# The two softmaxes of an attention unit: maximum, negation and exponential one softmax at a time

## The chip, the cores and the metric

The kernel runs on one core of a Trainium2 chip. The metric is the device time of one execution in microseconds (us); lower is better. The core has five engines that run side by side, each working through its own list of instructions in order: TensorE (PE: matmuls, with its weight loads PEld), VectorE (DVE), ScalarE (ACT), GpSimd (POOL) and SyncE (SP, which issues most loads). An instruction that needs another engine's result waits at the head of its engine's list, and all behind it wait too.

## The reference, cut to what matters

Two layers are applied to 640 tokens (512 latent ones and 128 context ones, 1024 wide). Each layer normalizes, projects to nine groups of 256 columns, runs four mixers side by side (differential attention, a gated short convolution, a gated recurrence, pooling), concatenates them, projects back, and then runs a squared-ReLU MLP. The change is in the differential attention of the latent tokens:

```python
def block(qi):
    s1 = jnp.einsum('bhqd,bhkd->bhqk', qi[..., :DK], k1).astype(jnp.float32) * scale
    s2 = jnp.einsum('bhqd,bhkd->bhqk', qi[..., DK:], k2).astype(jnp.float32) * scale
    p = jax.nn.softmax(s1, axis=-1) - lam * jax.nn.softmax(s2, axis=-1)
    return jnp.einsum('bhqk,bhkd->bhqd', p.astype(v.dtype), v)
```

There are 4 heads and 4 blocks of 128 queries, each against 640 keys (128 cached, 512 new): 16 units per layer, 32 in all, and each has two softmaxes over 640 keys.

## The kernel before

One function, `attn_unit`, records a unit. Four matmuls (L793) write both score blocks into one PSUM tile `S` of 128 x 1536, of which columns 128 to 768 are the first softmax and 768 to 1408 the second; there is one such tile. VectorE takes both row maxima in one instruction (L802) and multiplies the two by minus the scale in one more (L803), into columns of a small tile `mx`. ScalarE computes the two exponentials with that as bias (L806), each with its row sum, into two buffers of the pool `e`, which has three. VectorE then combines them (L810, L811, and L813 over 640 columns), which frees one `e`. TensorE transposes the result (L820, L825), ScalarE copies that out of PSUM (L827, L828), and after every second unit TensorE multiplies with the values (L840) and VectorE copies the output to `osb` (L845). After all units `attn_gen` squares the outputs (L882), sums them on TensorE (L885), takes the norm (L887 to L892), spreads it (L903), transposes it (L907), multiplies (L910) and splits the two halves of the attention output, `y[0]` and `y[1]`, into a high and a low part (L911, L912).

The other mixers and the large matmuls (L583, groups of 24 matmuls per result tile) run beside this. The projections of a layer come as `xr`, `gc`, `xb`, `xp`, `gr`, `gb`, each in four groups (0A, 1A, 0B, 1B), and after them the output projection `o`, whose groups go through `y[0]` to `y[7]` in order: `y[0]` and `y[1]` are the attention, `y[5]` ends with L639, `y[7]` with L1063. Weights are split into a high part on ScalarE (L260) and a low part on VectorE (L243).

All these pieces are Python generators that one loop advances in turn, and which buffer each takes is settled there, in the same way before and after the change. The order of instructions on each engine is then settled by a scheduler, which also puts in the waits between engines.

Of the kernel before, what the change touches and what calls it, by code (L numbers as in the profile page):

```python
# [12 lines left out]
OP = mybir.AluOpType  # L13
AX = mybir.AxisListType
# [100 lines left out]
class Net:  # L115
# [666 lines left out]
    def attn_unit(self, l, h, qt):  # L782
        nc = self.nc
        sc = 32.0 ** -0.5
        i = 4 * qt + h
        while not self.psS.ok():
            yield
        ps = self.psS.get()
        st = self.stacks[h]
        for s, parts in ((0, ((128, 0, 384), (512, 384, 640))), (1, ((768, 0, 256), (1024, 256, 640)))):  # L790
            Q, K = st[s]
            for o, a, b in parts:
                nc.tensor.matmul(ps[:, o:o + b - a], Q[:, qt * P:(qt + 1) * P], K[:, a:b], start=True, stop=True)  # L793
        if qt == 3:
            for s in range(2):
                self.z.put(*st[s])
        yield
        while not self.e.ok(2):
            yield
        mx = self.mx[self.mxi % 4]  # L800
        self.mxi += 1
        nc.vector.tensor_reduce(mx[:, 0:2], ps[:, 128:1408].rearrange("p (s k) -> p s k", s=2), AX.X, OP.max)  # L802
        nc.vector.tensor_scalar(mx[:, 2:4], mx[:, 0:2], -sc, None, OP.mult)  # L803
        es = [self.e.get(), self.e.get()]
        for s in range(2):
            nc.scalar.activation(es[s], ps[:, 128 + 640 * s:768 + 640 * s], AF.Exp, bias=mx[:, 2 + s:3 + s],  # L806
                                 scale=sc, accum_out=self.sm[:, i, s:s + 1])
        self.psS.put(ps)
        yield
        nc.vector.reciprocal(mx[:, 4:5], self.sm[:, i, 1:2])  # L810
        nc.vector.scalar_tensor_tensor(mx[:, 5:6], self.sm[:, i, 0:1], mx[:, 4:5], self.small[l][:, 4:5],  # L811
                                       OP.mult, OP.mult)
        nc.vector.scalar_tensor_tensor(es[0], es[1], mx[:, 5:6], es[0], OP.mult, OP.add)  # L813
        self.e.put(es[1])
        yield
        while not self.psA.ok():
            yield
        ta = self.psA.get()
        for kt in range(4):
            nc.tensor.transpose(ta[:, kt * P:(kt + 1) * P], es[0][:, kt * P:(kt + 1) * P], self.ident)  # L820
        yield
        while not (self.psB.ok() and self.pt.ok(2 - h % 2)):
            yield
        tb, pT = self.psB.get(), self.pt.get()
        nc.tensor.transpose(tb[:, 0:P], es[0][:, 512:640], self.ident)  # L825
        self.e.put(es[0])
        nc.scalar.copy(pT[:, 0:512], ta)  # L827
        nc.scalar.copy(pT[:, 512:640], tb[:, 0:P])  # L828
        self.psA.put(ta)
        self.psB.put(tb)  # L830
        self.pTs[h % 2] = pT
        if h % 2 == 0:
            return
        yield
        while not (self.v_done and self.psB.ok()):
            yield
        tb = self.psB.get()
        for kt in range(5):
            for j in range(2):
                nc.tensor.matmul(tb[64 * j:64 * j + 64, 0:P], self.vsb[:, kt, (h - 1 + j) * 64:(h + j) * 64],  # L840
                                 self.pTs[j][:, kt * P:(kt + 1) * P], start=(kt == 0), stop=(kt == 4),
                                 tile_position=(0, 64 * j))
        self.pt.put(*self.pTs)
        yield
        nc.vector.tensor_copy(self.osb[:, h // 2, qt * P:(qt + 1) * P], tb[:, 0:P])  # L845
        self.psB.put(tb)
# [764 lines left out]
```

## Time and profile before

| | us |
|---|---|
| median of 3 runs | 1493.53 (1489.97 to 1493.6) |
| the profiled execution | 1486.77 |
| its span in the trace | 1484.9 |
| PE busy | 1451.9 (98%) |
| DVE busy | 941.2 (63%) |
| ACT busy | 596.9 (40%) |
| POOL busy | 61.1 (4%) |

The span is what the trace covers; 1.87 us lie around it. The shares are means over stages that differ: the mixers of the first layer lie at about 62 to 250 us, those of the second at about 780 to 967 us, and the rest is mostly MLP. PE's busy time is modelled for pipelined matmuls, so that its idle time and the granted clock (PEclk, 1.00 is full speed) of a stretch say more than its share.

### The profile page before, as it was taken

What the parts mean: (1) busy time and instruction counts of PE and PEld (TensorE: products, weight loads), DVE (VectorE), ACT (ScalarE), POOL (GpSimd) and SP (SyncE); (2) the same over time, 40 slices, a digit from 0 to 9 for tenths busy, and PEclk for the clock granted to TensorE, in tenths of its full rate; (3) what the DMA queues carried; (4) which work ended last, traced back from release to release, by engine and by line L of the source; (5) the groups of instructions that cost most, each with busy time, mean ns of one, the idle gap of its engine ahead of it and who ended that gap; (6) DMA issues with size and microseconds to landing.
All of it is one profiled execution on the core that took longest, in us unless ns stands there. A gap on an engine that the chain in (4) does not pass through costs nothing.

```text
span 1484.9 us, 24604 instructions
## 1 busy us (share of the span) xinstructions
PE 1451.9 (98%) x9991; PEld 1388.0 (93%) x9991; DVE 941.2 (63%) x1846; ACT 596.9 (40%) x1083; POOL 61.1 (4%) x104
## 2 busy tenths in 40 slices
PE   8989999999999999999999999899999999999998
PEld 6867988999999999999999888799999999999997
DVE  5645888898886677776467678948533433433453
ACT  5435884453224133123344588625412312312331
POOL 1230010010000000000002200000000000000000
PEclk9999999999999999999999999999999999999999
DMA  9596013435554444544235501121222222221211
GB/s 336 173 245 184 22 46 89 142 109 165 186 170 130 153 145 140 170 128 128 71 90 129 132 17 58 59 71 57 86 86 72 71 86 67 76 86 59 84 44 72
DMA packets 135961, 164.59 MB, mean 111 GB/s; under 512 B 10212, under 2 KB 111032, under 8 KB 135848
## 3 DMA queue, kind: packets, MB, share of 16 engines
q1 hardware_dynamic: 128184, 151.69, 33.2%
q0 software_dynamic: 4224, 6.45, 1.9%
q10 hardware_dynamic: 3440, 4.88, 1.3%
q8 instruction: 79, 1.29, 0.4%
q14 instruction: 34, 0.28, 0.1%
HBM read 150.40 MB, written 3.15 MB: 103 GB/s over the span
## 4 chain that ended last, share of the span: by engine, by line
PE 83%; DVE 5%; DMA 5%; issue 4%; ACT 2%; ACTq 0%; DVEq 0%; POOLq 0%
PE g_L_0A L583 14%; PE g_L_1A L583 14%; PE g_L_0B L583 14%; PE g_L_1B L583 14%; PE g_L_o_0A L583 2%; DMA st<-in_w_in 2%; PE g_L_o_0B L583 2%; PE g_L_o_1B L583 2%; PE g_L_o_1A L583 2%; PE U L949 1%; PE S L793 1%; PE TB L840 1%; PE TA L820 1%; DMA st<-in_w_ada 1%; PE S L1501 1%
## 5 line engine op out<-in xcount | busy, mean ns | idle before, releaser
L260 ACT CAST wh<-st 128x1024 fp32r<-128x1024 f32 x180 | 188.8, 1049 | 336.1 <-PE g_L_1B L583 273.7
L243 DVE TENSOR_TENSOR wl<-st,wh 128x1024 fp32r<-128x1024 f32 x176 | 215.0, 1222 | 118.0 <-ACT wh L260 117.3
L1280 DVE TENSOR_TENSOR e<-e 128x320 f32<-128x320 f32 x128 | 62.5, 489 | 111.3 <-ACT z L1277 111.0
L583 PE MATMUL g_L_0A<-z,wh 128*128 128x320 f32 (+1 forms) x512 | 120.5, 313 | 0.6 <-DVE x L1220 0.4
L583 PE MATMUL g_L_1A<-z,wh 128*128 128x320 f32 (+1 forms) x512 | 120.9, 313 | 0.0
L583 PE MATMUL g_L_0B<-z,wh 128*128 128x320 f32 (+1 forms) x512 | 115.5, 306 | 0.3 <-DVE x L1220 0.3
L583 PE MATMUL g_L_1B<-z,wh 128*128 128x320 f32 (+1 forms) x512 | 115.1, 305 | 0.0
L305 DVE SCALAR_TENSOR_TENSOR m<-st,SC,m 128x512 f32<-128x512 f32 x112 | 79.6, 747 | 27.2 <-DMA st<-in_w_ada 27.2
L583 PEld LDWEIGHTS g_L_1A<-z,wh 128*128 128x128 f32 x512 | 87.5, 188 | 2.7 <-issue 2.5
L583 PEld LDWEIGHTS g_L_0A<-z,wh 128*128 128x128 f32 x512 | 87.7, 188 | 1.2 <-issue 1.1
L583 PEld LDWEIGHTS g_L_0B<-z,wh 128*128 128x128 f32 x512 | 86.2, 188 | 0.8 <-DVE x L1220 0.8
L583 PEld LDWEIGHTS g_L_1B<-z,wh 128*128 128x128 f32 x512 | 86.3, 188 | 0.1
L305 DVE SCALAR_TENSOR_TENSOR pt<-st,SC,pt 128x512 f32<-128x512 f32 x112 | 80.1, 747 | 2.2 <-DMA st<-in_w_ada 1.7
L583 PE MATMUL g_L_1A<-hh,wh 128*128 128x320 f32 x256 | 80.0, 312 | 0.0
L583 PE MATMUL g_L_0A<-z,wl 128*128 128x320 f32 (+1 forms) x256 | 79.8, 312 | 0.0
L583 PE MATMUL g_L_1A<-z,wl 128*128 128x320 f32 (+1 forms) x256 | 79.8, 312 | 0.0
L583 PE MATMUL g_L_0A<-hh,wh 128*128 128x320 f32 x256 | 79.5, 311 | 0.2
L583 PE MATMUL g_L_0B<-hl,wh 128*128 128x320 f32 x256 | 79.3, 310 | 0.0
L583 PE MATMUL g_L_1A<-hl,wh 128*128 128x320 f32 x256 | 79.2, 309 | 0.0
L583 PE MATMUL g_L_0A<-hl,wh 128*128 128x320 f32 x256 | 79.1, 309 | 0.0
L583 PE MATMUL g_L_1B<-hh,wh 128*128 128x320 f32 x256 | 79.1, 309 | 0.0
L583 PE MATMUL g_L_0B<-hh,wl 128*128 128x320 f32 x256 | 79.1, 309 | 0.0
(588 smaller groups left out, 3984.2 us busy)
## 6 DMA issues: line engine op xcount, KB each, us to landing
st<-in_w_mlp SPq DMA_DIRECT2D x128, 512.0 KB
st<-in_w_ada SPq DMA_DIRECT2D x80, 512.0 KB
st<-in_w_in SPq DMA_DIRECT2D x36, 512.0 KB
st<-in_w_out SPq DMA_DIRECT2D x16, 512.0 KB
z<-in_w_ada SPq DMA_DIRECT2D x24, 256.0 KB
z<-qk ACTq DMA_DIRECT2D x32, 80.0 KB
z<-qk POOLq DMA_DIRECT2D x32, 80.0 KB, 5.5
xt<-in_x_sample SPq DMA_DIRECT2D x4, 512.0 KB
```

The lines of the kernel that those rows point to most:

```text
L243: eng.tensor_tensor(wl.rearrange("p k c -> p (k c)"), st, wh.bitcast(F32).rearrange("p k c -> p (k c)"), OP.subtract)
L260: nc.scalar.copy(wh.rearrange("p k c -> p (k c)"), st)
L305: nc.vector.scalar_tensor_tensor(acc[:, 0:512], w, col, acc[:, 0:512], OP.mult, OP.add)
L583: nc.tensor.matmul(pt[:, 0:ncols], w[:, k % 4, sl], r, start=(n == 0), stop=(n == 23))
L793: nc.tensor.matmul(ps[:, o:o + b - a], Q[:, qt * P:(qt + 1) * P], K[:, a:b], start=True, stop=True)
L820: nc.tensor.transpose(ta[:, kt * P:(kt + 1) * P], es[0][:, kt * P:(kt + 1) * P], self.ident)
L840: nc.tensor.matmul(tb[64 * j:64 * j + 64, 0:P], self.vsb[:, kt, (h - 1 + j) * 64:(h + j) * 64], self.pTs[j][:, kt * P:(kt + 1) * P], start ...
L949: nc.tensor.matmul(u[:, 0:321], self.rgw[:, 4 * d + 2 * g + f, :], xc[:, cs], start=True, stop=True)
L1280: nc.vector.tensor_tensor(r[:, 0:n], r[:, 0:n], r[:, 0:n], OP.mult)
L1501: nc.tensor.matmul(acc[i][:, 0:self.wd(c)], w[:, k % 4, sl], x, start=(k == 0 and n == 0), stop=(k == KT - 1 and n == 2))
```

## The change

The joint maximum and the joint negation are taken apart. For each softmax in turn the unit records a maximum over its 640 columns, a negation of one column, and the exponential. The lines after this read the same values.

```diff
         mx = self.mx[self.mxi % 4]
         self.mxi += 1
-        nc.vector.tensor_reduce(mx[:, 0:2], ps[:, 128:1408].rearrange("p (s k) -> p s k", s=2), AX.X, OP.max)
-        nc.vector.tensor_scalar(mx[:, 2:4], mx[:, 0:2], -sc, None, OP.mult)
         es = [self.e.get(), self.e.get()]
         for s in range(2):
+            nc.vector.tensor_reduce(mx[:, s:s + 1], ps[:, 128 + 640 * s:768 + 640 * s], AX.X, OP.max)
+            nc.vector.tensor_scalar(mx[:, 2 + s:3 + s], mx[:, s:s + 1], -sc, None, OP.mult)
             nc.scalar.activation(es[s], ps[:, 128 + 640 * s:768 + 640 * s], AF.Exp, bias=mx[:, 2 + s:3 + s],
                                  scale=sc, accum_out=self.sm[:, i, s:s + 1])
```

The maximum is at L804 and the negation at L805 in the changed kernel. How the scheduler places them is seen on VectorE in the eighth unit of the first layer. Each row is one instruction: line, operation, output<-inputs (with the number that tells buffers apart), shape, and the engines whose progress it waits for. Before:

```order
L802 TENSOR_REDUCE mx_112<-S_1593 128x2 [waits PE_49]
L803 TENSOR_SCALAR mx_112<-mx_112 128x2 [waits DVE_49]
L1134 TENSOR_TENSOR m_29_1612<-g_L_xb_0A,m_25_1363 128x320 [waits PE_49]
L810 RECIPROCAL mx_112<-sm 128x1 [waits Activation_49]
L811 SCALAR_TENSOR_TENSOR mx_112<-sm,mx_112,small_107 128x1 [waits DVE_49]
L813 SCALAR_TENSOR_TENSOR e_23_1628<-e_24_1629,mx_112,e_23_1628 128x640 [waits DVE_49]
```

After, for the same buffers `e_23` and `e_24`:

```order
L804 TENSOR_REDUCE mx_112<-S_1603 128x1 [waits PE_49]
L805 TENSOR_SCALAR mx_112<-mx_112 128x1 [waits DVE_49]
L804 TENSOR_REDUCE mx_112<-S_1603 128x1 [waits Activation_49]
L805 TENSOR_SCALAR mx_112<-mx_112 128x1 [waits DVE_49]
L810 RECIPROCAL mx_112<-sm 128x1 [waits Activation_49]
L811 SCALAR_TENSOR_TENSOR mx_112<-sm,mx_112,small_107 128x1 [waits DVE_49]
L813 SCALAR_TENSOR_TENSOR e_23_1636<-e_24_1637,mx_112,e_23_1636 128x640 [waits DVE_49]
```

The second maximum waits for ScalarE; ScalarE's only work in the unit up to there is the first exponential, which reads the same tile `S`. That wait stands at the second maximum of all 32 units.

The second place is TensorE near the end of the first layer's mixers, around the transposes of the last unit (L820 x4 and L825). `gb_1A` and `gb_1B` are groups of the last projection, in the order 0A, 1A, 0B, 1B. Before:

```order
L583 MATMUL g_L_gb_1A<-hh,wh_2150 128x320
L583 MATMUL g_L_gb_1A<-hh,wl_2151 128x320
L820 MATMUL TA_2307<-cst,e_43_2265 128x128 x4
L825 MATMUL TB_2331<-cst,e_43_2265 128x128
L583 MATMUL g_L_gb_1A<-hl,wh_2150 128x320
L583 MATMUL g_L_gb_1A<-hh,wh_2150 128x320
```

After:

```order
L583 MATMUL g_L_gb_1B<-hh,wl_2242 128x320
L583 MATMUL g_L_gb_1B<-hl,wh_2241 128x320
L820 MATMUL TA_2339<-cst,e_43_2293 128x128 x4
L825 MATMUL TB_2363<-cst,e_43_2293 128x128
L840 MATMUL TB_2384<-pt_22_2289,vsb 64x128
L840 MATMUL TB_2384<-pt_23_2364,vsb 64x128
```

Before, 67 matmuls of `gb` stand behind the last transposes (19 of 1A, 24 of 0B, 24 of 1B); after, none. The same place in the second layer, before:

```order
L820 MATMUL TA_9758<-cst,e_188_9716 128x128 x4
L825 MATMUL TB_9782<-cst,e_188_9716 128x128
L583 MATMUL g_L_gb_0B<-hl,wh_9601 128x320
L583 MATMUL g_L_gb_0B<-hh,wh_9601 128x320
L583 MATMUL g_L_gb_0B<-hh,wl_9602 128x320
```

After:

```order
L820 MATMUL TA_9822<-cst,e_188_9776 128x128 x4
L825 MATMUL TB_9846<-cst,e_188_9776 128x128
L583 MATMUL g_L_gb_1B<-hh,wl_9725 128x320
L583 MATMUL g_L_gb_1B<-hl,wh_9724 128x320
L840 MATMUL TB_9867<-pt_63_9772,vsb 64x128
```

There 43 matmuls of `gb` stand behind them before (19 of 0B, 24 of 1B), and 2 after.

## Rows read from the trace of the kernel before

**Rows 1.** The page's first part: busy us, share, instructions.
```profile
PE 1451.9 (98%) x9991; PEld 1388.0 (93%) x9991; DVE 941.2 (63%) x1846; ACT 596.9 (40%) x1083; POOL 61.1 (4%) x104
```
**Rows 2.** Stretches: length, busy us (instructions) by engine, clock, DMA share, GB/s.
```profile
160.00:180.00 20.00, 19.93 (x155) 18.46 (x155) 19.54 (x47) 15.94 (x31) 0.00 (x0) 1.00 0.00 1
...
220.00:240.00 20.00, 17.01 (x126) 15.50 (x124) 17.14 (x41) 12.30 (x22) 1.55 (x2) 0.93 0.26 61
...
940.00:960.00 20.00, 16.45 (x110) 14.82 (x109) 17.61 (x42) 12.66 (x22) 1.92 (x3) 0.85 0.26 80
...
1040.00:1060.00 20.00, 20.00 (x138) 20.00 (x137) 10.69 (x17) 8.96 (x17) 0.00 (x0) 1.00 0.33 106
```
**Rows 3.** PE in order of time: start, us, what, count, idle before and its releaser.
```profile
219.58 0.63 PE L820 MATMUL TA<-cst,e 128*128 128x128 f32 x4 [0.51 <-DVE e L813]
...
240.16 0.63 PE L583 MATMUL g_L_o_0A<-z,wh 128*128 128x320 f32 x1 [1.72 <-ACT z L911]
...
938.92 0.63 PE L820 MATMUL TA<-cst,e 128*128 128x128 f32 x4 [0.53 <-DVE e L813]
...
956.39 0.64 PE L583 MATMUL g_L_o_0A<-z,wh 128*128 128x320 f32 x1 [1.28 <-ACT z L911]
```
**Rows 4.** The chain that ended last: start, us, what; one group of 24 matmuls.
```profile
249.89 3.52 PE g_L_o_0B L583 x24
```
**Rows 5.** Groups by form, VectorE, the unit: busy us, mean ns, idle before and releaser.
```profile
L802 DVE TENSOR_REDUCE mx<-S 128x2 f32<-128x1280 f32 x32 | 47.5, 1485 | 5.1 <-PE S L793 4.9
...
L803 DVE TENSOR_SCALAR mx<-mx 128x2 f32<-128x2 f32 x32 | 5.2, 163 | 0.2
```
**Rows 6.** Groups by form, ScalarE, the exponentials.
```profile
L806 ACT ACTIVATE e<-S,mx 128x640 f32<-128x640 f32 x64 | 50.7, 800 | 6.3 <-DVE mx L803 2.3 <-DVE e L753 2.1 <-PE g_L_xb_0A L583 1.5
...
L806 ACT ACTIVATION_READ_ACCUMULATOR e<-S,mx 128x1 f32 x64 | 13.1, 205 | 0.0
L806 ACT ACT_TABLE_LOAD x7 | 9.0, 1283 | 0.1
```
**Rows 7.** VectorE's waits, 100 to 240 us: us, times, longest.
```profile
DVE mx L810 <- ACT e L806: 15.1, 7, 7.6
DVE mx L802 <- PE S L793: 3.9, 3, 1.9
DVE osb L845 <- PE TB L840: 3.3, 2, 2.1
DVE m L1145 <- PE g_L_gb_1A L583: 1.8, 1, 1.8
```
**Rows 8.** VectorE's waits, 820 to 968 us.
```profile
DVE mx L810 <- ACT e L806: 9.9, 7, 2.4
...
DVE osb L845 <- PE TB L840: 3.5, 3, 1.4
DVE fin L888 <- PE TB L885: 2.1, 1, 2.1
DVE z L1063 <- ACT z L1062: 1.2, 1, 1.2
DVE m L956 <- ACT m L953: 1.1, 1, 1.1
```
**Rows 9.** Groups by form, VectorE, steps of other mixers near the end.
```profile
L1010 DVE SCALAR_TENSOR_TENSOR m<-e,m 128x640 f32<-128x640 f32 x4 | 3.3, 818 | 0.0
...
L1047 DVE SCALAR_TENSOR_TENSOR m<-m,cst,m 128x512 f32<-128x512 f32 x4 | 3.0, 745 | 0.0
...
L1045 DVE TENSOR_TENSOR m<-m,cst 128x8 f32<-128x8 f32 x16 | 1.7, 160 | 0.0
...
L1047 DVE SCALAR_TENSOR_TENSOR m<-m,cst,m 128x128 f32<-128x128 f32 x4 | 1.4, 345 | 0.0
L1014 DVE SCALAR_TENSOR_TENSOR m<-z,m 128x512 f32<-128x512 f32 x2 | 1.4, 684 | 0.0
```
**Rows 10.** A short stretch at the end of the first layer's mixers.
```profile
242.00:244.00 2.00, 2.00 (x8) 1.87 (x7) 1.71 (x3) 0.53 (x1) 0.00 (x0) 0.50 0.00 0
```

## The prediction

> **What bounds the kernel now.** I read the page's shares first, then the stretches of 20 us, then TensorE in order of time where its share falls, then who VectorE waits for, and last the groups by form for prices. TensorE is busy for 98% of the span [rows 1], and in the MLP for all of it, as in the stretch from 1040 us [rows 2], so only stages in which it waits can give or take time. They lie at the end of each layer's mixers: 17.01 and 16.45 of 20 us [rows 2]. What ends those waits is the attention. In the first layer TensorE waits 0.51 us for the last unit's combination (L813) at 219.58, and 1.72 us for the second half of the attention output (L911) at 240.16; in the second layer 0.53 us and 1.28 us, at 938.92 and 956.39 [rows 3]. VectorE stands behind both: from 160 to 180 us it is busy for 19.54 of 20 us, though over the span only for 63% [rows 1, 2]. So work on VectorE is cheap over the span as a whole and dear in the second half of each mixer stage. Before, the last units end just in time; the `gb` groups that stand behind them on TensorE cover the closing steps of the attention.
>
> **What the change adds on VectorE.** Per unit it takes away one maximum of 1.485 us and one negation of 0.163 us [rows 5] and adds two of each. No row shows a maximum over 640 columns here. It can't cost under half, 0.743 us, nor more than the whole, 1.485 us. I take the one-column negation's 0.163 us as the part that does not shrink: (1.485 - 0.163)/2 + 0.163 = 0.824 us, since the time of these steps is otherwise read elements. So a unit costs 2 x 0.824 + 2 x 0.163 - 1.485 - 0.163 = 0.33 us more, and a layer's 16 units 5.2 us. The ends are 2.6 us (half) and 26 us (whole) per layer.
>
> **What it adds in waits.** It does not overlap what it seems to. The second maximum waits for the first exponential in every unit, as the order shows, since both read the tile `S`. So per unit VectorE can now stop twice, for about 1.1 us each (0.800 us for the exponential and 0.205 us for its row sum [rows 6], and a crossing), where before it could stop once for 2.1 us (L810 behind both). Behind it are queued the low parts of weights (L243), the other mixers and the next unit. What hides such a wait is other VectorE work that stands between. I added up the mean durations by form of the instructions that the order puts there. Before, 19.0 us are not hidden in the 32 units; the trace shows 25.0 us, 15.1 and 9.9 [rows 7, 8], 1.3 times as much. After, 13.1 us are not hidden ahead of the second maxima (18 of 32 have too little in front) and 12.4 us ahead of L810, together 25.5. That is 6.5 us more, or 8.6 us by the factor; I take 7.5, 3.75 per layer. The ends: if every second maximum is hidden after all, 12.4 x 1.3 - 25.0 = -9 us for both layers; if each waits a whole exponential and L810 stays as it is, +32 us. ScalarE gets one more pair of table loads, 2 x 1.283 us [rows 6], around the first layer's eighth unit; it is busy for 15.94 of 20 us there [rows 2], so I cost them at nothing, and at 2.6 us if that slack is used up.
>
> **What moves.** The scheduler places the last units later against the large matmuls, and puts other steps ahead of the attention's closing steps on VectorE. In the first layer L1010 (0.818), one L1014 (0.684) and one L1047 (0.345) now stand before the last step of `y[1]`: 1.85 us. In the second it is four L1045 (1.7/16 = 0.11 each), one L1010 and one L1047 (0.745): 2.0 us [rows 9].
>
> **What takes some of it up.** VectorE also waits for things that don't depend on this: 3.9 + 3.3 + 1.8 = 9.0 us for TensorE in the first layer [rows 7], and 3.5 + 2.1 + 1.2 + 1.1 = 7.9 us in the second [rows 8]. Whatever comes later runs in such gaps. None or all of it may serve; I take half, 4.5 and 4.0 us, since some of these gaps wait for the attention itself (L802, L845, L888) and move with it.
>
> **First sum**, at the point where `y[1]` is there: 5.2 + 3.75 + 1.85 - 4.5 = 6.3 us in the first layer and 5.2 + 3.75 + 2.0 - 4.0 = 7.0 us in the second, together 13.3 us. Behind that point the same matmuls of `o` remain in both kernels; `y[5]` and `y[7]` get only the 5.2 us of work and are late by less than `y[1]`.
>
> **Second sum, by TensorE's cover.** A matmul of a full group costs 3.52/24 = 0.147 us [rows 4]. Before, 67 of them (9.8 us) stand behind the last transposes in the first layer and 43 in the second; after, 0 and 2. So the last transposes come 9.8 and 41 x 0.147 = 6.0 us later, if TensorE gets there unhindered. From them to the second half it took 240.16 - 219.58 = 20.6 us and 956.39 - 938.92 = 17.5 us [rows 3], for the most part VectorE's queue. In that queue, by the same mean durations, the work between the last L813 and the end of `y[1]` falls from 22.6 to 18.5 us and from 21.2 to 18.8 us. So `y[1]` is late by 9.8 - 4.1 = 5.7 and 6.0 - 2.4 = 3.6 us, together 9.3 us. This leaves out waits, as the first sum leaves out TensorE. I take 11 us, between the two. TensorE's clock was down to 0.50 at the end of the first layer's mixers [rows 10], the lower of its two levels, after it had waited for the attention. I expect one such spell per layer as before, at no more cost; if it starts sooner, the closing matmuls (L820, L840, L885, L907; 0.63 us for the first [rows 3]) may take twice as long, about 2.5 us per layer.
>
> The profiled execution took 1486.77 us, 0.45% under the median of 1493.53. The sums are differences within it: 1486.77 + 11 = 1497.8 us in such an execution, and 1493.53 + 11 = 1504.5 us against the median, which I forecast.
>
> **Rivals.** *No change* (1494.5 us). The gaps of 9.0 and 7.9 us take up nearly all of 5.2 + 3.75 + 2 = 11 us per layer. For it speaks that the cover is only lost if the attention is late, and that VectorE has time earlier in the stage; against it that the order has already moved the last units behind the cover, so that TensorE gets to them later even if VectorE is in time.
>
> *Faster* (1487.5 us). The first exponential starts 1.485 - 0.824 = 0.66 us sooner, so `S` and the `e` buffers come free sooner, and each unit's loop gets shorter. It would win TensorE's waits, 0.51 + 1.72 + 0.53 + 1.28 = 4.0 us [rows 3], and part of the spell at the low clock that follows them, some 2 us. It decides if the last L813 ends before 219.5 and 938.8 us. Against it: with the wait the second exponential ends no sooner than 2 x (0.824 + 0.163 + 1.005) = 3.98 us after the scores, against 1.648 + 2 x 1.005 = 3.66 before. The Trainium skill has a rule for this side: Perfetto Trace Analysis, section Optimizing Scalar/DVE Operations, says that where Scalar and Vector aren't saturated but cause bubbles on other engines, breaking up instructions may let work end sooner, and also that larger operations improve throughput where the engine is saturated. By the 63% of the whole span the first half of it would hold, and the time would be this rival's; by the 19.54 of 20 us the second half holds, and the time is the forecast's.
>
> *Two engines in step* (1527 us). If every second maximum waits a whole exponential, the 3.75 us per layer become 16 us, and no gap is left to take up the delay: 5.2 + 16 + 2 - 6 = 17 us per layer. It decides if VectorE's waits at the second maximum add up to over 25 us. Against it speak the 14 of 32 units with enough work in between.
>
> **Chances.** Forecast 0.68, no change 0.17, faster 0.08, in step 0.07. A measurement of this kernel can tell about 0.3% from no change, 4.5 us. So slower by more has 0.68 + 0.07 = 0.75, within it 0.17, faster 0.08. The range goes from 1494, half of the no-change case, to 1517: the second sum without its shortening is 9.8 + 6.0 = 15.8 us, and with 8.6 us of waits 24 us. It leaves out faster, half of no change, and in step.
>
> **What would show it.** In the changed kernel's profile: L804 64 times at about 0.82 us and L805 64 times at 0.16; VectorE waiting for L806 both at L804 and at L810, together some 33 us; the last L820 of each layer behind the `gb` groups, and TensorE nearly idle for 8 to 15 us from there to `o`; the first `o` matmul on `y[1]` 4 to 8 us later in the first layer and, from the start of its own mixers, in the second; the MLP unchanged at 3.52 us a group. The forecast is wrong if the last L813 of each layer ends where it did, or if the maximum over 640 columns costs far from 0.82 us; the mechanism is wrong if the time is lost in the MLP or before the second unit.

## The result, and the profile after

The changed kernel takes 1509.08 us (median; 1504.89 to 1511.08), the kernel before 1491.75 us on the same chip. The ratio is 1.0115, 95% interval 1.0085 to 1.0145: slower by 17 us, where 1504.5 us (11 us slower) was forecast. The profiled execution took 1504.89 us, with a span of 1503.0 us.

The page's first part of the changed kernel, to be read against [rows 1]: busy us, share, instructions.

```profile
PE 1456.6 (97%) x9991; PEld 1392.5 (93%) x9991; DVE 948.2 (63%) x1910; ACT 600.7 (40%) x1085; POOL 60.9 (4%) x104
```

VectorE has 64 instructions more and 7.0 us more work, and its share hasn't moved: on this line the change can't be seen. The stretches show it (length, busy us by engine, granted clock, DMA share, GB/s; against [rows 2]):

```profile
220.00:240.00 20.00, 16.36 (x127) 15.34 (x125) 18.91 (x43) 15.41 (x27) 1.55 (x2) 1.00 0.04 11
240.00:260.00 20.00, 15.11 (x82) 13.60 (x82) 19.55 (x40) 10.19 (x16) 1.20 (x2) 0.74 0.13 34
...
880.00:900.00 20.00, 14.66 (x79) 12.33 (x79) 16.00 (x34) 17.45 (x28) 0.00 (x0) 0.74 0.18 54
...
960.00:980.00 20.00, 12.02 (x83) 10.24 (x82) 18.63 (x45) 12.64 (x22) 1.90 (x3) 0.74 0.35 53
...
1060.00:1080.00 20.00, 20.00 (x138) 20.00 (x138) 9.88 (x16) 8.81 (x16) 0.00 (x0) 1.00 0.34 106
```

The MLP (last line) is full as before. TensorE loses time at both closings, as forecast, and in a third place that was not forecast, in the middle of the second layer's mixers. In order of time on TensorE (against [rows 3]; start, us, what, idle before and its releaser):

```profile
234.44 0.63 PE L820 MATMUL TA<-cst,e 128*128 128x128 f32 x4 [2.17 <-DVE e L813]
244.14 1.12 PE L907 MATMUL TA<-cst,e 128*128 128x128 f32 x4 [4.13 <-DVE e L903]
...
250.26 0.52 PE L583 MATMUL g_L_o_0A<-z,wh 128*128 128x320 f32 x1
...
889.14 1.09 PE L820 MATMUL TA<-cst,e 128*128 128x128 f32 x4 [1.26 <-DVE mx L805]
892.91 0.63 PE L583 MATMUL g_L_xp_0A<-hh,wh 128*128 128x320 f32 x1 [2.47 <-DVE mx L805]
...
961.35 0.63 PE L820 MATMUL TA<-cst,e 128*128 128x128 f32 x4 [0.17 <-DVE e L813]
971.25 1.12 PE L907 MATMUL TA<-cst,e 128*128 128x128 f32 x4 [4.13 <-DVE e L903]
978.15 0.42 PE L583 MATMUL g_L_o_0A<-z,wh 128*128 128x320 f32 x1 [0.48 <-ACT z L911]
985.47 0.31 PE L583 MATMUL g_L_o_0B<-z,wh 128*128 128x320 f32 x1
```

Before, TensorE still had `gb` groups to do behind the last L820; now it goes straight to the closing steps and waits 4.13 us for L903 in each layer; the first `o` matmul on `y[1]` stands at 250.26 and 978.15 us (240.16 and 956.39 before). At 892.91 us a group of `xp` waits 2.47 us. The view names the negation (L805) that ends at that moment, but `xp_0A` doesn't read it. What ends 0.06 us before it is the step that empties the tile of `xb_1B` (L1134); these groups share two PSUM tiles, and in the second and sixth experiments the view names that step itself as the releaser of `xp_0A`. VectorE in order of time:

```profile
891.30 0.35 DVE L1134 TENSOR_TENSOR m<-g_L_xb_1B,m 128x192 f32<-128x192 f32 x1
891.83 0.83 DVE L804 TENSOR_REDUCE mx<-S 128x1 f32<-128x640 f32 x1 [0.18 <-ACT e L806]
892.57 0.28 DVE L1134 TENSOR_TENSOR m<-g_L_xb_1B,m 128x128 f32<-128x128 f32 x1
```

The matmuls of `xb_1B` were done at 881.47 us; before, the same step began 0.21 us after them (878.71 against 878.50). So VectorE comes to it some 10 us late: the order puts maxima, a combination (L813), the splitting of weights (L243) and steps of other mixers ahead of it, and a second maximum in its middle.

The unit's instructions by group (busy us, mean ns, idle before and releaser; against [rows 5, 6]):

```profile
L804 DVE TENSOR_REDUCE mx<-S 128x1 f32<-128x640 f32 x64 | 52.5, 820 | 28.9 <-ACT e L806 22.5 <-PE S L793 5.6
L805 DVE TENSOR_SCALAR mx<-mx 128x1 f32<-128x1 f32 x64 | 9.5, 148 | 0.7
L810 DVE RECIPROCAL mx<-sm 128x1 f32<-128x1 f32 x32 | 5.0, 157 | 12.6 <-ACT e L806 12.5
```
```profile
L806 ACT ACTIVATE e<-S,mx 128x640 f32<-128x640 f32 x64 | 51.1, 799 | 19.3 <-DVE mx L805 14.4 <-DVE e L753 2.4 <-DVE m L1084 1.9
L806 ACT ACT_TABLE_LOAD x8 | 10.3, 1283 | 0.1
```

The two engines now wait for each other: VectorE for the exponentials 22.5 + 12.5 = 35.0 us (25.0 before), ScalarE for the negation 14.4 us (2.3 before).

What these groups don't show is how long one unit keeps the score tile `S`, the only one there is. Here is the tenth unit of the first layer. Its scores (L793) start at 180.66 us on TensorE. VectorE in order of time:

```profile
182.24 0.82 DVE L804 TENSOR_REDUCE mx<-S 128x1 f32<-128x640 f32 x1
182.98 0.88 DVE L813 SCALAR_TENSOR_TENSOR e<-e,mx,e 128x640 f32<-128x640 f32 x1
183.77 0.14 DVE L805 TENSOR_SCALAR mx<-mx 128x1 f32<-128x1 f32 x1
183.83 0.88 DVE L931 SCALAR_TENSOR_TENSOR z<-m,PT,z 128x642 f32<-128x642 f32 x1
184.63 0.84 DVE L1031 TENSOR_TENSOR m<-m 128x663 f32<-128x663 f32 x1
185.39 0.81 DVE L804 TENSOR_REDUCE mx<-S 128x1 f32<-128x640 f32 x1
186.12 0.88 DVE L931 SCALAR_TENSOR_TENSOR z<-m,PT,z 128x642 f32<-128x642 f32 x1
186.91 0.15 DVE L805 TENSOR_SCALAR mx<-mx 128x1 f32<-128x1 f32 x1
```

and ScalarE and TensorE:

```profile
183.95 0.80 ACT L806 ACTIVATE e<-S,mx 128x640 f32<-128x640 f32 x1
...
187.16 0.80 ACT L806 ACTIVATE e<-S,mx 128x640 f32<-128x640 f32 x1
```
```profile
180.66 0.74 PE L793 MATMUL S<-z,z 128*128 128x384 f32 x4
...
188.48 0.74 PE L793 MATMUL S<-z,z 128*128 128x384 f32 x4
```

No row of VectorE has idle time before it. The scheduler has filled the wait for the exponential with steps of other mixers (L931, L1031), and put another L931 between the second maximum and its negation. So VectorE loses nothing, and the unit does: its second exponential starts 3.21 us after the first. `S` is taken from 180.66 to 187.96 us, 7.30 us, and the next scores start at 188.48. The same unit before, on TensorE, VectorE and ScalarE:

```profile
169.16 0.85 PE L793 MATMUL S<-z,z 128*128 128x384 f32 x4
...
170.88 1.49 DVE L802 TENSOR_REDUCE mx<-S 128x2 f32<-128x1280 f32 x1
...
173.27 0.80 ACT L806 ACTIVATE e<-S,mx 128x640 f32<-128x640 f32 x1 [0.74 <-DVE mx L803]
...
174.06 0.79 ACT L806 ACTIVATE e<-S,mx 128x640 f32<-128x640 f32 x1
...
175.21 0.75 PE L793 MATMUL S<-z,z 128*128 128x384 f32 x4
```

There the two exponentials stand back to back (0.95 us apart on the mean of the first layer), and `S` is taken for 5.69 us.

Read in this way for all 16 units of a layer (from the first L793 of a unit to the end of its second exponential, from the timelines of TensorE and ScalarE), `S` was taken for 6.46 and 6.78 us a unit before, in the first and the second layer, and for 7.52 and 7.67 us after. Between one unit's second exponential and the next unit's scores lie 0.1 to 0.5 us in 22 of 30 cases before and 25 of 30 after; most of the longer pauses are in the first layer. So the units stand in a queue at `S`, and the last one is late by 16 times what one unit keeps it longer, less what the pauses give back (in the first layer 0.74 us on the mean before, 0.49 after). From a layer's first scores to its last exponential it took 114.4 and 113.4 us before, and takes 127.6 and 128.6 us after. This is the theory **buffer**. Its rivals: **work** (VectorE's added work sets the end), **stops** (VectorE's time at L804 is what costs, called wait in the first expectations), and the forecast's **cover** (what counts is how many matmuls the order leaves behind the last L820).

### The profile page after: what moved, and what is told of

Read it like the earlier page. It is cut to its first block, busy times and chain, and to the rows that moved or that the text cites. A ratio compares the mean times of both kernels' runs of the same rounds, so it can differ in the third digit from the quotient of the medians.

```text
span 1503.0 us, 24688 instructions
## 1 busy us (share of the span) xinstructions
PE 1456.6 (97%) x9991; PEld 1392.5 (93%) x9991; DVE 948.2 (63%) x1910; ACT 600.7 (40%) x1085; POOL 60.9 (4%) x104
## 4 chain that ended last, share of the span: by engine, by line
PE 83%; DVE 6%; DMA 5%; issue 4%; ACT 2%; POOL 0%; ACTq 0%; DVEq 0%; POOLq 0%; SPq 0%
PE g_L_0A L583 14%; PE g_L_1A L583 14%; PE g_L_0B L583 13%; PE g_L_1B L583 13%; PE g_L_o_1A L583 2%; DMA st<-in_w_ada 1%; PE g_L_o_0A L583 1%; PE g_L_o_0B L583 1%; PE g_L_o_1B L583 1%; PE S L793 1%; DMA st<-in_w_in 1%; PE TB L840 1%; PE U L949 1%; PE g_L_v L1177 1%; PE TA L820 1%
## 5 line engine op out<-in xcount | busy, mean ns | idle before, releaser
L243 DVE TENSOR_TENSOR wl<-st,wh 128x1024 fp32r<-128x1024 f32 x176 | 214.9, 1222 | 121.1 <-ACT wh L260 120.7
L583 PE MATMUL g_L_0A<-hh,wl 128*128 128x320 f32 x256 | 79.1, 309 | 0.0
L583 PE MATMUL g_L_0B<-hh,wh 128*128 128x320 f32 x256 | 79.1, 309 | 0.0
```

What stands on the lines that cost most here:

```text
L243: eng.tensor_tensor(wl.rearrange("p k c -> p (k c)"), st, wh.bitcast(F32).rearrange("p k c -> p (k c)"), OP.subtract)
L583: nc.tensor.matmul(pt[:, 0:ncols], w[:, k % 4, sl], r, start=(n == 0), stop=(n == 23))
```

## The experiments

All ratios are to the kernel before on the same chip. "Span at S" is the time from a layer's first scores to its last exponential, first and second layer; "kept" is the mean time for which a unit keeps `S`.

| kernel | ratio, interval | span at S, us | kept, us |
|---|---|---|---|
| before, control | 1 | 117.1, 113.3 | 6.58, 6.77 |
| changed | 1.0115 (1.0085 to 1.0145) | 127.6, 128.6 | 7.52, 7.67 |
| 1 work only | 0.9956 (0.9941 to 0.9972) | 108.8, 107.5 | 6.09, 6.38 |
| 2 wait only | 1.0095 (1.0079 to 1.0110) | 128.8, 119.8 | 7.59, 7.19 |
| 3 cover only | 1.0045 (1.0032 to 1.0057) | 126.1, 115.8 | 6.47, 6.49 |
| 4 cover back | 1.0238 (1.0216 to 1.0259) | 122.0, 118.5 | 7.04, 7.00 |
| 5 held longer | 1.0020 (1.0009 to 1.0031) | 116.2, 112.3 | 6.12, 6.06 |
| 6 second at once | 1.0092 (1.0073 to 1.0111) | 130.4, 118.1 | 7.72, 7.03 |
| 7 negation alone | 0.9971 (0.9958 to 0.9985) | 109.6, 112.4 | 6.15, 6.73 |
| 8 short second | 1.0015 (1.0002 to 1.0029) | 121.2, 112.8 | 7.02, 6.82 |
| 9 second layer | 1.0068 (1.0051 to 1.0085) | 115.4, 128.4 | 6.54, 7.65 |
| 10 joint, early | 0.9966 (0.9951 to 0.9980) | 108.6, 106.6 | 5.81, 6.18 |
| 11 split, early | 1.0016 (1.0002 to 1.0030) | 111.1, 106.3 | 6.02, 6.12 |

**Control.** The kernel before, unchanged.

> The kernel before once more, for its trace. In the profiles of the changed kernel and of the four experiments so far the first scores of the first layer come at 104.2 to 105.6 us, in the one profile of before at 102.03, though no instruction ahead of that point is changed. If this is chance between executions, a second profile of before lies between 102 and 105.6 there, its time within 0.3% of 1492; if it is not chance, at 102.0 again, and 2.6 us of the loss lie ahead of the attention.

It took 1493.04 us, and its trace has on TensorE:

```profile
102.86 1.01 PE L793 MATMUL S<-z,z 128*128 128x384 f32 x4 [0.45 <-issue]
...
223.15 0.63 PE L820 MATMUL TA<-cst,e 128*128 128x128 f32 x4 [0.51 <-DVE e L813]
244.67 0.63 PE L583 MATMUL g_L_o_0A<-z,wh 128*128 128x320 f32 x1 [1.86 <-ACT z L911]
```

The first scores come at 102.86 us, between the 102.03 of the first profile and the changed kernel's 104.67, so a part of these 2.6 us is chance. And the same instructions end the first layer's mixers 4.5 us later than in the first profile ([rows 3]: 244.67 against 240.16). One profile of a layer is good to some 4 us here; the second layer, counted from its own first scores, repeats to 0.2 us (144.49 and 144.32 us to `o_0B`).

**1, work only.** Against the changed kernel:

```diff
         for s in range(2):
             nc.vector.tensor_reduce(mx[:, s:s + 1], ...)
             nc.vector.tensor_scalar(mx[:, 2 + s:3 + s], ...)
+        for s in range(2):
             nc.scalar.activation(es[s], ...)
```

> Both half maxima and both negations come ahead of both exponentials, so the second maximum waits for no exponential. VectorE's work is that of the changed kernel (two maxima of 820 ns and two negations of 148 ns per unit, +9.3 us over the kernel before), and the order now leaves 108 and 85 matmuls of `gb` groups on TensorE behind the last L820 of the two layers (67 and 43 before, 0 and 2 after). Forecast's theory (the time is lost where TensorE runs out of cover): 41 and 42 matmuls more of cover are worth 6 us per layer against 4.7 us of work, so ratio to before 0.997 to 1.002. Rival work (VectorE's work in the mixers sets the end): +9 us, 1.006. Rival wait (only the crossing between the engines costs): 1.000, whatever the cover.

Faster than before, by 6.6 us at 0.9956, and 24 us below the changed kernel at the same work on VectorE. Its groups:

```profile
L804 DVE TENSOR_REDUCE mx<-S 128x1 f32<-128x640 f32 x64 | 50.7, 817 | 5.9 <-PE S L793 5.8
L805 DVE TENSOR_SCALAR mx<-mx 128x1 f32<-128x1 f32 x64 | 8.9, 146 | 0.1
L811 DVE RECIPROCAL mx<-sm 128x1 f32<-128x1 f32 x32 | 5.1, 159 | 22.6 <-ACT e L807 22.6
```

No maximum waits for ScalarE. The ratio lies below all three forecasts, that of cover (0.997 to 1.002) too. The rival work is out: the 9 us that it adds cost nothing here.

**2, wait only.** Against the changed kernel, the second maximum reads columns 768 to 1131:

```diff
-ps[:, 128 + 640 * s:768 + 640 * s]
+ps[:, 128 + 640 * s:768 + 363 * s]
```

> As the changed kernel, but the second maximum reads only 363 of its 640 columns (any shift that keeps the exponentials finite gives the same softmax), so that a unit's two maxima and negations cost VectorE about as much as before: 820 + 530 + 2 x 148 = 1646 ns against 1485 + 163. The wait of the second maximum for the first exponential stays. The order leaves 0 and 30 matmuls of cover behind the last L820 (67 and 43 before). Forecast's theory: without the 4.7 us of work per layer, with the waits and with 67 and 13 matmuls less of cover, 9.8 + 1.9 us less what is gained behind them: ratio 1.004 to 1.008. Rival work: 1.000. Rival wait: the whole loss, 1.010 to 1.012.

1.0095: most of the loss with none of the added work. This was above what the theory of cover gave (1.008 at most), and just under the range of the rival wait.

**3, cover only.** Against the kernel before:

```diff
-                    wait = 3
+                    wait = 4
```

> The kernel before with one number changed: the attention's generator lets 4 turns instead of 3 pass between the starts of two units. No instruction is changed, added or taken away. The order leaves 24 and 6 matmuls of cover behind the last L820 (67 and 43 before, 0 and 2 after). Forecast's theory (cover decides): 43 x 0.147 = 6.3 us and 37 x 0.147 = 5.4 us later at the last transposes, less some that the closing steps give back: +5 to +10 us, ratio 1.003 to 1.007. Rivals work and wait, both: 1.000, since neither is changed.

1.0045, as the theory of cover had it; work and wait had nothing to change here. So units that come late cost time with no instruction changed. The unit keeps `S` as long as before (6.47 and 6.49 us), but the pauses between units grow, to 1.51 us on the mean in the first layer (0.79 in the control), and from a layer's first scores the last exponential comes 9.0 and 2.4 us later than in the control.

**4, cover back.** Against the changed kernel:

```diff
-                    wait = 3
+                    wait = 1
```

> The changed kernel with one number changed: 1 turn instead of 3 between the starts of two units. Every instruction of the change stays (work and wait). The order leaves 66 and 11 matmuls of cover behind the last L820 (67 and 43 before, 0 and 2 after). Forecast's theory: the first layer's loss at its end goes (within 2 us of before), the second layer's shrinks by 9 x 0.147 = 1.3 us at the close and keeps its stall in the middle: ratio 1.004 to 1.008. Rivals work and wait: unchanged, 1.0115.

A miss for all three: 1.0238, slower than the changed kernel, though its units end sooner after a layer's first scores. TensorE's largest waits in the whole span:

```profile
PE U L1060 <- DVE m L1047: 11.7, 2, 7.3
PE g_L_o_0A L583 <- ACT z L1148: 8.5, 2, 4.7
```

Now the pooling mixer is last (L1047), and with it steps of the `gb` evacuation (L1148): 20.2 us. VectorE's queue is shared, and what the attention takes earlier the others get later. Counting matmuls behind the last L820 says nothing on this; the theory of cover can hold only while the attention is last.

**5, held longer.** Against the kernel before:

```diff
-        self.psS.put(ps)
         yield
         nc.vector.reciprocal(mx[:, 4:5], self.sm[:, i, 1:2])
+        nc.vector.tensor_copy(mx[:, 8:9], ps[:, 1407:1408])
+        self.psS.put(ps)
```

> The kernel before (joint maximum, joint negation, both exponentials) with one copy of a single column of the score tile `S` on VectorE behind each unit's first reciprocal (L810), its result unused. It keeps the only score buffer taken until VectorE has come that far; 32 copies of about 0.15 us, 4.8 us in all. Order: 66 and 70 matmuls of cover behind the last L820 (67 and 43 before). Theory hold (new, from the traces: per unit the time from its first maximum to the end of its second exponential grew from 5.07 and 5.36 us before to 6.13 and 6.45 us after, 17 us per layer, and the next unit's scores wait for that buffer): buffer held about 1 us longer per unit, last combinations 5 to 12 us later per layer, ratio 1.003 to 1.010. Theory cover (the forecast's second sum): 1.000 or under. Rival work: 4.8 us at most, and by the experiment with the work alone nothing: 0.998 to 1.003.

1.0020, below what the theory of the buffer gave and in the range of work, but it did not lengthen what it should. The scheduler put less other work into the units, so that the exponentials ended sooner (6.12 and 6.06 us), and with the copy and the pause behind it a unit's turn took 7.34 and 7.08 us, in the control 7.37 and 7.10. So it tells nothing on the theory of the buffer.

**6, second at once.** The changed kernel, with its two rounds of maximum, negation and exponential under

```diff
+        with self.tc.high_priority(offset=40):
```

> The changed kernel, with the two maxima, negations and exponentials of a unit issued at a higher priority (offset 40), so that the scheduler puts less other VectorE work between the first negation and the second maximum. Cover 0 and 22 matmuls (0 and 2 after). Theory hold: the buffer is held 0.5 to 1 us shorter per unit than in the changed kernel (6.13 and 6.45 us there), last combinations earlier by 5 to 12 us per layer though VectorE waits longer at L804 in sum: ratio 1.002 to 1.008. Theory wait (VectorE's stops count as lost time of VectorE, as in the forecast's first sum): L804's waits grow over 22.5 us, ratio 1.0115 or more. Theory cover: 1.009 to 1.0115.

1.0092, in the range of cover and above that of the buffer. It did half of what it should: kept falls to 7.03 us in the second layer and rises to 7.72 us in the first. The spans at `S` add up to 7.7 us less than in the changed kernel, and the time is some 3 us less, within the intervals. The maxima's waits for ScalarE did not grow (21.6 us, 22.5 in the changed kernel), so the theory of stops got neither the longer waits nor the ratio that it asked for, and the buffer got its shorter units in one layer only: this doesn't decide between them.

**7, negation alone.** Against the kernel before:

```diff
-        nc.vector.tensor_scalar(mx[:, 2:4], mx[:, 0:2], -sc, None, OP.mult)
         for s in range(2):
+            nc.vector.tensor_scalar(mx[:, 2 + s:3 + s], mx[:, s:s + 1], -sc, None, OP.mult)
             nc.scalar.activation(es[s], ...)
```

> The maximum stays joint; only the negation is done for one softmax and then for the other, each ahead of its exponential. Of the change this leaves 32 more negations of 0.148 us (4.6 us in both layers) and no wait of VectorE for ScalarE within a unit, since the negation doesn't read `S`. Cover 99 and 46 matmuls (67 and 43 before). Theory hold: held as before (5.1 to 5.4 us), ratio 0.998 to 1.002. Theory cover: 32 x 0.147 = 4.7 us earlier in the first layer, 0.996 to 0.998. Rival work: +4.6 us, 1.003.

0.9971: this part of the change is no loss, rather a small gain. That is in the range of cover and below the other two; `S` was not kept as before, as the theory of the buffer had assumed, but 0.43 and 0.04 us shorter than in the control. So what costs is the second maximum.

**8, short second.** As the second experiment, with 16 columns in place of 363.

> As the second experiment, but the second maximum reads only 16 of its 640 columns (the shift differs, the softmax doesn't). All 32 second maxima still wait for the first exponential, with other VectorE work ordered in between, 1.8 us a unit by mean durations (1.9 in the changed kernel). Cover 45 and 38 matmuls. Theory buffer (new: the units stand in a row at the one score buffer, gaps of 0.1 to 0.5 us, so the last unit comes 16 occupancies after the first; from the first score matmul to the end of the second exponential 6.46 and 6.78 us before, 7.52 and 7.67 after): occupancy 0.6 us shorter than in the changed kernel, 6.9 and 7.0, last exponentials 113 to 119 us after the first scores (127.6 and 128.6 after), ratio 1.000 to 1.005. Theory stops (what costs is that VectorE stops at L804 for ScalarE): L804's waits stay at 22 to 28 us, ratio 1.008 to 1.0115.

1.0015. Its two forms of maximum:

```profile
L804 DVE TENSOR_REDUCE mx<-S 128x1 f32<-128x640 f32 x32 | 26.2, 819 | 4.5 <-PE S L793 4.5
...
L804 DVE TENSOR_REDUCE mx<-S 128x1 f32<-128x16 f32 x32 | 5.5, 170 | 23.4 <-ACT e L806 23.1
```

VectorE stops at the second maximum as long as in the changed kernel (23.1 against 22.5 us), and at L810 too (13.0 against 12.5), and nearly the whole loss is gone. So the stops are not what costs. `S` is kept for 7.02 and 6.82 us, a little high in the first layer and back at before's in the second; the ratio is in the range of the buffer, and the spans at `S`, 113 to 119 us by it, came out at 121.2 and 112.8. Against the second experiment it saves 32 x (531 - 170) ns = 11.6 us of the second maximum, which stands between the two exponentials, and 0.8% of the time, 12 us. Both differ in VectorE's work as well, but in the first experiment more work of the same kind, ahead of both exponentials, cost nothing. Between buffer and cover this run doesn't decide: 27 matmuls less of cover than before would be 4.0 us, at 0.147 us each [rows 4].

**9, second layer.** The change for `l == 1` alone.

> The change in the second layer alone; the first layer keeps the joint form. Cover 67 and 2 matmuls. By the trace of the changed kernel the second layer loses most: from its first scores to o's second half 154.94 us against 144.49 and 144.32 in the two profiles of before, 10.5 us, some of it in a stall at 884 to 899 us that the forecast didn't have: ratio 1.006 to 1.008. By the forecast's two sums 7.0 or 3.6 us: 1.002 to 1.005. If the layers don't add (the second layer's stall depends on what the first one left late): under 1.003.

1.0068, 10.1 us, as the traces said and above the forecast's two sums. The stall in the middle comes back without the change in the first layer:

```profile
889.84 0.64 PE L583 MATMUL g_L_xp_0A<-hh,wh 128*128 128x320 f32 x1 [2.76 <-DVE mx L806]
```

For the first layer this leaves some 0.5%, 7 us, as a difference.

**10, joint, early, and 11, split, early.** The kernel before, and the first experiment, with a unit's maximum, negation and exponentials under `high_priority(offset=40)`.

> The kernel before, joint, with the maximum, negation and exponentials of a unit issued at a higher priority (offset 40); no instruction is added or taken away. Cover 120 and 99 matmuls. Theory buffer: less other VectorE work stands between a unit's scores and its maximum, occupancy 5.9 to 6.3 us, last exponentials under 110 us after the first scores; TensorE's waits at the close (6.4 us in the second profile of before, first layer) mostly go: ratio 0.993 to 0.997. Rival (the other mixers, pushed behind, stand last instead, as in the fourth experiment where TensorE waited 7.3 us for L1047): 1.000 to 1.020.

> The first experiment (both half maxima and negations ahead of both exponentials) with the same higher priority (offset 40). Cover 134 and 112 matmuls. Theory buffer: occupancy under the first experiment's 6.09 and 6.38 us, last exponentials under 107 us after the first scores; of the first experiment's waits of TensorE (2.0 us in the first layer's mixers, some 9 in the second's) a few go: ratio 0.992 to 0.9955. Rival (other mixers last): 1.000 to 1.020.

The spans at `S` are short in both. The tenth kernel is faster than before by 0.34%, in the range of the buffer; the eleventh, which differs from it by the split alone, is slower by 0.16%, in the range of the rival. In it TensorE waits in both layers for the steps of `xb` on VectorE that the attention was put ahead of:

```profile
PE g_L_xb_1B L583 <- DVE m L1136: 2.7, 2, 2.0
...
PE g_L_xp_0A L583 <- DVE m L1136: 2.2, 1, 2.2
```

The second row is the stall in the middle again, in a kernel in which no second maximum stands behind an exponential. Where TensorE waits for others, a shorter span at `S` buys nothing more. The lowest ratio of all has the first experiment, but its interval overlaps with those of the seventh and the tenth.

## Why the prediction was right, and where not

**The direction and the range** held: slower, 1509.08 us in a range of 1494 to 1517. The size was 11 us against 17. By the ninth experiment 7 us of this belong to the first layer, about what the two sums gave for it (6.3 and 5.7), and 10 us to the second, where they gave 7.0 and 3.6. The working behind it is wrong in one step.

**Sizes of work.** The maximum over 640 columns takes 820 ns (0.824 worked out), the negation 148 ns (0.163). VectorE's work for the unit grew by (52.5 + 9.5) - (47.5 + 5.2) = 9.3 us (10.4). Right in size, but the first sum counted it as 5.2 us per layer of lateness, and the first experiment shows that by itself it costs nothing.

**Sizes of waits.** L804 and L810 together wait 35.0 us for the exponentials ("some 33 us"). Right in size too, and again counted as what it is not: the eighth experiment keeps these stops and loses 0.15%. The one more pair of table loads (L806 has 8 against 7) shows no cost of its own: the eighth experiment has 8 too.

**The step that failed** is "What hides such a wait is other VectorE work that stands between", with the sum over what was not hidden. Such work hides the wait for VectorE and not for the unit. The rival *faster* had the unit's own bound, 3.98 us from scores to the end of the second exponential against 3.66, 0.3 us more; it was set against that rival and then left out of the sum. With the hiding work in between it became 1.06 and 0.89 us per unit, and since there is one score tile, the last exponential came 13.2 and 15.2 us later, over a layer's 16 units and the pauses between them (10.5 and 15.3 against the control), where the first sum had 5.2 us of work and 3.75 us of waits per layer. Less the 4.7 us of added work, the term that was sized at 3.75 us is some 6 to 9 us in the first layer and 10.5 us in the second. In the mean unit of the first layer the first exponential starts 0.75 us sooner after the first maximum (2.57 against 3.32 us), and the second 1.81 us later after the first (1.02 + 1.74 against 0.95).

VectorE waits 22.5 us at L804 behind L806, though both only read `S`. The Trainium skill (PSUM — Partial Sum Buffer, section PSUM bank collisions raise a hardware error) says that two engines may not be in one bank and quadrant at once, two readers neither, and that software has to keep them apart. The trace shows such a wait, but not that the bank is its reason: no run here separates the bank from the tile.

**Cover.** It was lost as the order showed, and lateness costs as the third experiment has it (1.0045 with no change of instructions). The second sum's terms can be read off, counted from a layer's first scores. The last L820 comes 12.2 us later than in the first profile in the first layer (9.5 against the control) and 14.7 us later in the second, where 9.8 and 6.0 were forecast. From there to `o` on `y[1]` it takes 4.8 us less (5.7) and 0.7 us less, where 4.1 and 2.4 were forecast. So this sum came out in the first layer and failed in the second. The take-up by VectorE's gaps (4.5 and 4.0 us) was no separate gain that a run shows. In the first layer `o` on `y[1]` starts 10.1 us later than in [rows 3] and 5.6 us later than in the control (250.26 against 240.16 and 244.67), of which 2.6 and 1.8 us were there at the first scores (104.67 against 102.03 and 102.86): 7.5 and 3.8 us, about the 4 to 8 forecast. In the second layer, from its own first scores, it starts 13.9 us later (978.15 - 830.53 = 147.62 against 963.13 - 829.37 = 133.76 us). There the forecast is out, by the step that failed and by the stall in the middle.

**TensorE nearly idle for 8 to 15 us.** Not quite borne out. From the last L820 to `o` on `y[1]` lie 15.8 and 16.8 us, and TensorE is idle for 6.0 and 7.8 us of them (before, 3.1 of 20.6 and 3.6 of 17.5):

```profile
234.44:250.26 15.82, 9.80 (x64) 8.01 (x64) 14.72 (x35) 9.78 (x16) 1.55 (x2) 0.68 0.06 10
961.35:978.15 16.80, 8.99 (x63) 7.61 (x64) 15.43 (x36) 10.62 (x19) 1.90 (x3) 0.70 0.42 64
```

**One spell at the low clock per layer.** Two in the second layer: behind the stall in the middle too the granted clock was 0.50, the lower of its two levels:

```profile
890.00:892.00 2.00, 0.44 (x3) 0.03 (x1) 1.82 (x4) 1.72 (x5) 0.00 (x0) 0.50 0.02 5
892.00:894.00 2.00, 1.09 (x4) 1.09 (x5) 1.46 (x8) 1.97 (x3) 0.00 (x0) 0.50 0.00 0
894.00:896.00 2.00, 2.00 (x9) 2.00 (x8) 2.00 (x3) 1.99 (x3) 0.00 (x0) 0.50 0.00 0
```

TensorE had been busy for 0.44 of the 2 us from 890 on, and was full from 894 on, at 0.50. 19 matmuls of `xp_0A` took 5.4 us; at 0.147 us each [rows 4] it would have been 2.8. The last group of `gb` then ends 4.9 us later after the layer's first scores (131.5 against 126.6 us), so about half of that layer's 10.5 us arise here. As far as the rows show, this half is not the queue at `S` itself but VectorE's order, which brings the step for `xb_1B` late; no run changed that alone. The stall is there in the second layer of experiments 2, 4, 6, 9 and 11, and not of 1, 7 and 8.

**The MLP** is unchanged: a full group takes 3.52 us as in [rows 4].

```profile
432.50 3.52 PE g_L_1A L583 x24
```

**Rivals.** No change and faster are out by the interval, two engines in step by its own condition: L804 waits 22.5 us, under 25. The rule weighed beside the rival *faster* (the Trainium skill, Perfetto Trace Analysis, section Optimizing Scalar/DVE Operations) was decided by VectorE's share in the stage: saturated, so larger operations. The runs don't bear that out as a rule: with smaller operations in the same saturated stage the work ended sooner in the first experiment (0.9956), and with the higher priority later (the eleventh, 1.0016, against the tenth, 0.9966). Between the changed kernel and the first experiment, with the same operations, what decided was where the second maximum stood.

**What stays open.** Why the order of the first experiment has shorter turns at `S` than the joint form (6.09 and 6.38 against 6.58 and 6.77 us), though its maxima and negations together take 1.93 us against 1.65, was not separated from the scheduler's choices. And buffer and order were never changed one without the other; a second score tile was not tried. So cover is not out as a rival while the attention is last: a longer span at `S` mostly goes with fewer matmuls behind the last L820. What speaks for the span is that experiments 2 and 3 both leave 30 of them in the two layers and take 1.0095 and 1.0045, with 248.6 and 241.9 us at `S` in sum.

## What to carry to other kernels

Where all units of a loop pass through one buffer, price an edit by how long a unit keeps that buffer, times the units, not by the busy or idle time of an engine: work that hides a wait for the engine lengthens it for the unit. Splitting a reduction cost little or nothing here with both halves ahead of the engine that reads the result (a gain of 0.44% in one pair of runs, a loss of 0.5% in another), and 1.15% with the second half behind it. When the last chain of a stage is made earlier, look at which one is last then.

## What the runs showed of the hardware

A row maximum over columns of PSUM took 170 ns for 16 columns (experiment 8), 531 for 363 (experiment 2), 820 for 640 (changed) and 1485 for 1280 (before): about 1.04 ns a column and 153 ns beside them, so two halves cost 155 ns more than the whole. At the granted clock of 0.50 the 19 matmuls of `xp_0A` mostly took 0.27 us from one start to the next; at 1.00, in the stretch from 1060 us, 138 matmuls fill 20 us, 0.145 us each.
